# Triangular inverses of eight token tiles in one bundle, and planner estimates read off the trace

## The chip, the cores and the metric

The kernel runs on one core of one Trainium2 chip. The metric is the device time of one execution in microseconds. Its engines are named as the profile names them: PE (TensorE, with PEld for its weight loads), DVE (VectorE), ACT (ScalarE), POOL (GpSimd) and SP (SyncE, which here only issues DMAs). Each engine works through its own instructions in order, and engines wait for each other by semaphores.

## What is computed

One layer of a hybrid backbone: 1024 latent tokens and 256 context tokens of width 1024 are normed and projected, three mixers run on the projection (a gated linear recurrence, LRU; a gated delta rule, GDN; a state-space scan, SSD), their outputs are merged and projected, and a mixture of experts follows. The change lies in the GDN, whose core is, for a chunk of tokens of one head:

```python
dec = jnp.exp(jnp.where(incl, gcs[..., :, None] - gcs[..., None, :], -jnp.inf))
kb = kc * bc[..., None]
a_low = jnp.where(strict, jnp.einsum("bhid,bhjd->bhij", kb, kc) * dec, 0.0)
rhs = jnp.concatenate([vc * bc[..., None], kb * jnp.exp(gcs)[..., None]], axis=-1)
sol = lax.linalg.triangular_solve(eye + a_low, rhs, left_side=True, lower=True, unit_diagonal=True)
u, w = sol[..., :dv], sol[..., dv:]
v_new = u - jnp.einsum("bhcd,bhde->bhce", w, s)
o = (jnp.einsum("bhcd,bhde->bhce", qc * jnp.exp(gcs)[..., None], s)
     + jnp.einsum("bhij,bhje->bhie", attn, v_new))
s = s * jnp.exp(gcs[..., -1])[..., None, None] + jnp.einsum("bhcd,bhce->bhde", k_dec, v_new)
```

Eight heads are scanned in both directions, first over the context (from a zero state), then over the latents (from the context's final state). The kernel takes chunks of 128 tokens and replaces the triangular solve by the inverse of `I + B`, with `B` the strictly triangular matrix of a token tile and a direction.

## The kernel before

**Stages.** The stages follow each other: start (norms, transposes), LRU with the context's projections beside it (to about 586 us), GDN over the context (to 765), SSD (to 1268), GDN over the latents (to 2135), the merge and the output projection (to 2640), the experts. A stage's pools are opened and closed with it, and `drain` ends it.

**The order of work.** The main line of a stage is a list of jobs (`run`, line 350): projections of one block of 128 channels, each 48 products of 512 columns in single-precision-round format (`pj`). All else is side work, written as generators in the list `post`. After every three products (of a half block's row tile) `tick` (393) walks through `post` and lets each generator run to its next `yield`, if the planner's clock says that its last step is done. That order is fixed when the program is built: instructions go to the engines in it.

**The planner's clock.** `Clock` (145) holds an estimated time for each engine and each tile. `issue` (190) starts an instruction at the latest of its engine's time, its inputs' and its output buffer's, and adds `cost` (164). "Now" is TensorE's estimated time. A result counts as ready 0.1 us after its instruction. Costs before: a 512-column projection product 512 / 2400 = 0.213 us, a small single-precision product at least 0.06 us, a VectorE instruction 0.07 us (0.13 from PSUM) and 1.05 ns an element, for copies 0.53 ns; a scan counts as any other. `room` (386) waits for a PSUM bank by estimate, `take` (421) for a buffer by count, `until` holds up the main line for a flag, with the clock moved on to the next side step.

**GDN over the latents.** A head has two batches (`Batch`) of four token tiles. `gdn_jobs` (1583): the blocks K, Q, V of heads 0 and 1 are projected first; then for each head h its scans are added (`gdn_chain`, 1513, one generator a direction, eight steps each) and its output (`gdn_out`), the gate block GZ of h is projected, the main line waits for head h - 1's output, and K, Q, V of head h + 2 follow; a few merge gate blocks fill heads 5 to 7. `gdn_pre` of a head runs after that of the head before and after its K: for each batch `gdn_keys` (transposed keys, norms `sk`, factors `D`), `gdn_decays` (1192: POOL masks `gm`, two pairs of products `parg`, decays `dec`, `at` from queries, and, when a buffer `B` is free, eight DVE instructions `B<-pkk,D,dec` and two POOL masks), and then a side task `gdn_inverse` for that batch. After both batches it makes the values `vp` and sets `gpre`. A scan waits for the scan before, for `gpre` and for the inverses of both batches (`gi`).

**The inverse** (1267), for four token tiles in both directions at once: the diagonal 32-blocks of `B` go into `Bq`; the 16-blocks are inverted by substitution, 15 rounds of two shuffles of rows (`R<-Y`), a product (`R<-R,Bc`) and a difference (`Y<-Y,R`), all on DVE, in widths from 1 to 15 columns; then blocks are merged 16 to 32 to 64 to 128, each by two sets of small products on PE with copies by ACT and DVE between (`p1`, `py`, `p2`, `po` and `pz`, `p3`, `p4`; in the trace `p` and `P`). The result lies in `Yf`. Buffers for the latents: two of `B`, each given back after its inverse's `p3`; one of `Bq`, given back after `Bo`, ahead of the merges; one of `Yq`, given back at the end. The context works alike with batches of one token tile of four heads, and has two sets of buffers (`pars`), so two inverses at a time.

Of the kernel before, what the change touches and what calls it, by code (L numbers as in the profile page):

```python
# [136 lines left out]
CH2 = True  # L137
# [7 lines left out]
class Clock:  # L145
    """Estimated times (us) at which the engines and the tiles are free of the instructions issued so far; the order
    in which independent pieces of work are issued goes by them."""

    TABLES = (("Tanh", "Exp"), ("Gelu_apprx_tanh", "Tanh"), ("Silu", "Tanh"), ("Sqrt",), ("Sigmoid", "Tanh"))

# [67 lines left out]
class TimedPool:  # L218
    """a tile pool; keeps book of when the buffers that its tiles take over are free."""
# [50 lines left out]
class Core:  # L270
# [15 lines left out]
    # ---------------------------------------------------------------- consts  # L286
# [24 lines left out]
    def softplus(self, out, x, pool, shape, name):  # L311
        """max(x, 0) + log(1 + exp(-|x|)), the logarithm as 2 atanh(e / (2 + e))."""
# [39 lines left out]
    def run(self, jobs):  # L352
        """jobs: callables, or (weight block, kind, done); done(block, psum tile, is latent)."""
# [19 lines left out]
    def give(self, ps):  # L373
        """a projection's PSUM tile is not needed any more."""
# [754 lines left out]
    def gdn_fixed(self):  # L1129
# [4 lines left out]
        for y in self.Yf + self.Z64:  # L1134
            nc.vector.memset(y, 0.0)
# [1381 lines left out]
```

## Time and profile before

| | us |
|---|---|
| median of 3 runs | 3391.51 |
| lowest and highest | 3386.56, 3393.18 |
| span of the profiled execution | 3387.1 |

The profile is of one execution. The span runs from its first to its last instruction; the time of a run holds some microseconds around it (the median is 4.4 above this span). In the rows below, "busy" is the time in which an engine had an instruction under way, "idle before" what it stood ahead of the instructions of a group, with the engine and tile that ended it. Nearly all instructions carry line 256, that of the wrapper that records them, so tiles tell them apart. A single-precision product appears as two records. A tile's name is that of the program without its number: `p1`, `p2`, `p3` and `p4` are `p`, and `P1`, `P2`, `P3` are `P`.

### The profile page before, as it was taken

What the parts mean: (1) busy time and instruction counts of PE and PEld (TensorE: products, weight loads), DVE (VectorE), ACT (ScalarE), POOL (GpSimd) and SP (SyncE); (2) the same over time, 40 slices, a digit from 0 to 9 for tenths busy, and PEclk for the clock granted to TensorE, in tenths of its full rate; (3) what the DMA queues carried; (4) which work ended last, traced back from release to release, by engine and by line L of the source; (5) the groups of instructions that cost most, each with busy time, mean ns of one, the idle gap of its engine ahead of it and who ended that gap; (6) DMA issues with size and microseconds to landing.
All of it is one profiled execution on the core that took longest, in us unless ns stands there. A gap on an engine that the chain in (4) does not pass through costs nothing. (4 is left out here: it accounts for less than half of the span.)

```text
span 3387.1 us, 48583 instructions
## 1 busy us (share of the span) xinstructions
PE 2976.2 (88%) x18570; PEld 2345.0 (69%) x18570; DVE 2251.0 (66%) x5049; ACT 1553.5 (46%) x2188; POOL 772.1 (23%) x662
## 2 busy tenths in 40 slices
PE   7878789879799789879989999899988799999992
PEld 3657667667568557668777778677766588878882
DVE  4676765753744745887988885244544887787786
ACT  4556565424315324454444444311121576676674
POOL 1121221202612611112111111212110243333333
PEclk8989999979799799989999999999989799999996
DMA  4112222201002001001010111454443697887896
GB/s 187 63 56 78 74 76 78 78 24 50 13 32 75 7 26 62 28 21 35 22 34 27 34 47 65 153 195 174 150 145 136 260 361 290 310 337 287 321 354 235
DMA packets 105531, 423.12 MB, mean 125 GB/s; under 512 B 17224, under 2 KB 26568, under 8 KB 79696
## 3 DMA queue, kind: packets, MB, share of 16 engines
q1 hardware_dynamic: 79872, 372.17, 30.5%
q10 hardware_dynamic: 13968, 26.83, 2.1%
q0 software_dynamic: 11456, 21.00, 1.7%
q8 instruction: 147, 2.41, 0.3%
q14 instruction: 88, 0.72, 0.1%
HBM read 381.11 MB, written 59.79 MB: 130 GB/s over the span
## 5 line engine op out<-in xcount | busy, mean ns | idle before, releaser
L256 PE MATMUL pj<-hhi,whi 128*128 128x512 f32 x1488 | 643.8, 433 | 17.8 <-DVE kq L256 10.3
L256 PE MATMUL pj<-hhi,wlo 128*128 128x512 f32 x1488 | 597.7, 402 | 6.9 <-POOL wlo L256 3.7
L256 PE MATMUL pj<-hlo,whi 128*128 128x512 f32 x1488 | 597.4, 401 | 0.0
L256 DVE TENSOR_TENSOR wl<-raw,wh 128x2048 fp32r<-128x2048 f32 x188 | 447.9, 2403 | 103.4 <-ACT wh L256 101.1
L256 POOL TENSOR_TENSOR wlo<-raw,whi 128x1024 fp32r<-128x1024 f32 x78 | 197.1, 2527 | 1002.8 <-ACT whi L256 985.5
L256 ACT ACTIVATE wh<-raw 128x2048 fp32r<-128x2048 f32 x188 | 360.6, 1919 | 129.2 <-PE psu L256 103.2
L256 PEld LDWEIGHTS pj<-hhi,whi 128*128 128x128 f32 x1488 | 286.7, 193 | 77.8 <-issue 10.1
L256 PEld LDWEIGHTS pj<-hhi,wlo 128*128 128x128 f32 x1488 | 285.3, 192 | 78.4 <-POOL wlo L256 5.3
L256 PEld LDWEIGHTS pj<-hlo,whi 128*128 128x128 f32 x1488 | 287.6, 193 | 53.8 <-issue 3.2
L256 ACT ACTIVATE whi<-raw 128x1024 fp32r<-128x1024 f32 x145 | 152.8, 1056 | 293.6 <-PE pj L256 212.8
L256 PE MATMUL psu<-wl,xh 128*128 128x512 f32 x576 | 226.6, 393 | 2.9 <-DVE wl L256 2.9
L256 PE MATMUL psu<-wh,xh 128*128 128x512 f32 x576 | 229.1, 398 | 0.0
L256 PE MATMUL psu<-wh,xl 128*128 128x512 f32 x576 | 226.0, 392 | 1.1 <-DVE xl L256 1.1
L256 ACT ACT_TABLE_LOAD x147 | 188.6, 1283 | 77.0 <-DVE xt L256 32.2
L256 DVE TENSOR_TENSOR wlo<-raw,whi 128x1024 fp32r<-128x1024 f32 x67 | 87.8, 1310 | 185.0 <-ACT whi L256 185.0
L256 ACT ACTIVATE w<-ch,D 128x128 f32<-128x128 f32 x288 | 84.7, 366 | 161.6 <-PE ch L256 155.7
L256 POOL TENSOR_TENSOR yo<-yo,m 128x1024 f32<-128x1024 f32 x35 | 103.6, 2961 | 183.5 <-ACT yo L256 183.4
L256 PE MATMUL psg<-u,lw 128*128 128x512 f32 (+1 forms) x192 | 89.8, 605 | 55.5 <-issue 52.7
L256 PE MATMUL pj<-bh,whi 128*128 128x512 f32 x384 | 122.9, 402 | 12.0 <-DVE acc L256 6.5
L256 PE MATMUL pj<-bl,whi 128*128 128x512 f32 x384 | 122.2, 400 | 8.9 <-POOL bl L256 6.3
L256 PEld LDWEIGHTS psu<-wl,xh 128*128 128x128 f32 x576 | 109.0, 189 | 29.3 <-DVE wl L256 8.0
L256 PEld LDWEIGHTS psu<-wh,xl 128*128 128x128 f32 x576 | 108.8, 189 | 24.7 <-DVE xl L256 1.8
(455 smaller groups left out, 6295.5 us busy)
## 6 DMA issues: line engine op xcount, KB each, us to landing
raw<-in_w SPq DMA_DIRECT2D x188, 1024.0 KB, 6.8
raw<-in_w_in SPq DMA_DIRECT2D x119, 512.0 KB, 3.5
wr<-in_w_mod SPq DMA_DIRECT2D x32, 512.0 KB, 6.0
gate<-gt ACTq DMA_DIRECT2D x48, 256.0 KB, 2.0
raw<-in_w_branch SPq DMA_DIRECT2D x24, 512.0 KB, 3.6
st<-br SPq DMA_DIRECT2D x24, 512.0 KB, 5.5
gt<-gate SPq DMA_DIRECT2D x24, 512.0 KB, 4.5
wm<-in_w_mod SPq DMA_DIRECT2D x8, 1024.0 KB, 5.7
```

The source lines that it names most:

```text
L256: return f(*args, **kw)
```

## The change

`gdn_inverse` takes both batches of a head (in the context, both token tiles of four heads), so that each of its instructions covers eight token tiles. `gdn_pre` adds it once, after the keys and decays of both batches. The tiles double in their third dimension, and there is one set: `B` two buffers, both given back after `p3`; `Bq`, `Bo`, `Yq` and `Zq` one each, shared by what was in `Bc`, `Y`, `R` and `P1`; `Bq` is taken at the start and given back at the end. `Z64` holds one direction for each quadrant, so half of the `pz` products and of the copies around them go. `Bo` is made ahead of the substitution, a yield comes after every second round instead of every third, and `p4` waits for a bank. `small_tiles` keeps one tile less, and the switch `CH2` goes (its branch stays for the latents). `Clock.cost` gets new lines, and the lag after an instruction depends on its engine.

```diff
+    LAG = {"tensor": 0.21, "vector": 0.11, "scalar": 0.12, "gpsimd": 0.1, "sync": 0.1}
...
         if eng == "tensor":
             if op == "transpose":
-                return 0.12
+                return 0.11
             c = kw["rhs"].free_size()
-            return c / 2400 if kw["rhs"].dtype == F32R else max(4 * c / 2400, 0.06)
+            if kw["rhs"].dtype == F32R:
+                return c / 2400 + 0.014
+            rows = kw["lhsT"].partition_size()
+            if "tile_position" in kw:
+                return 0.024 if rows == 32 else 0.055
+            return max(c / 600, 0.11)
+        psum = any(a.space == PSUM for a in ins)
         if eng == "vector":
             if op == "reciprocal":
                 return 0.07 + n * 6.3e-3
+            if op == "tensor_tensor_scan":
+                return 0.08 + n * 2.08e-3
             if op == "tensor_reduce":
-                n = ins[0].free_size()
-            psum = any(a.space == PSUM for a in ins)
-            fast = op in ("tensor_copy", "tensor_scalar") and not psum
-            return (0.13 if psum else 0.07) + n * (0.53e-3 if fast else 1.05e-3)
+                return 0.08 + ins[0].free_size() * 1.04e-3
+            if op == "stream_shuffle":
+                return 0.13 + n * 1.0e-3
+            if op in ("tensor_copy", "tensor_scalar", "memset"):
+                c = 0.14 if len(ins) > 1 else 0.09
+                return c + n * (1.04e-3 if psum else 0.52e-3)
+            c = 0.15 if op == "scalar_tensor_tensor" and len(ins) > 2 else 0.09
+            return c + n * 1.04e-3
         if eng == "scalar":
             f = str(kw.get("func")).split(".")[-1]
-            c = 0.13 + 0.75e-3 * n
+            c = (0.08 if psum else 0.12) + 0.09 * max(0, len(ins) - 1) + 0.83e-3 * n
+            if kw.get("accum_out") is not None:
+                c += 0.2
             if any(f in t for t in self.TABLES) and f not in self.table:
                 self.table = next(t for t in self.TABLES if f in t)
-                c += 1.28
+                c += 1.38
             return c
         if op == "indirect_dma_start":
             return 1.0
-        return 0.1 + n * {"tensor_tensor": 2.2e-3, "affine_select": 1.05e-3}.get(op, 3.5e-3)
+        if op == "affine_select":
+            return 0.12 + n * 0.9e-3
+        return 0.15 + n * (2.25e-3 if op == "tensor_tensor" else 3.5e-3)
...
-            t += 0.1
+            t += self.LAG[eng]
...
-        self.pars = 1 if lat else 2
-        b |= {f"{n}{p}": 2 if n == "B" and lat else 1 for p in range(self.pars)
-              for n in ("B", "Bq", "Bo", "Bc", "Y", "R", "Yq", "Zq", "P1")}
+        b |= {"B": 2} | dict.fromkeys(("Bq", "Bo", "Yq", "Zq"), 1)
...
         for bt in bts:
             yield from self.gdn_keys(bt, keys=not lat)
             yield from self.gdn_decays(bt)
-            self.add(self.gdn_inverse(bt))
+        self.add(self.gdn_inverse(bts))
...
+        def t(name, c):
+            return g.tile([P, 2, 8, c], F32, tag=name, name=name)
...
+        yield from self.take(g, "Bq")
+        Bq = t("Bq", 32)
+        for i, bt in enumerate(bts):
+            for q in range(4):
+                r = slice(32 * q, 32 * q + 32)
+                o = Bq[r, :, 4 * i:4 * i + 4, :]
...
+        Bc = flat(t("Zq", 32))[:, 0:256].rearrange("p (d e c) -> p d e c", d=2, c=16)
...
+        yr = flat(t("Bq", 32)).rearrange("p (n d e c) -> p n d e c", n=2, d=2, c=16)
+        Y, R = yr[:, 0], yr[:, 1]
...
-            nc.vector.tensor_tensor(out=Rv, in0=Rv, in1=Bv, op=ALU.mult)
+            Rv, Yv = Rw[:, :, j:], Yw[:, :, j:]
+            nc.vector.tensor_tensor(out=Rv, in0=Rv, in1=Bw[:, :, j:j + 1].to_broadcast([P, 16, 16 - j]), op=ALU.mult)
             nc.vector.tensor_tensor(out=Yv, in0=Yv, in1=Rv, op=ALU.subtract)
-            if s % 3 == 2:
+            if s % 2:
                 yield
...
-                nc.tensor.matmul(pz[rb, e, :], lhsT=Y32[rb, d, e, :], rhs=P2[rb, e, :], start=True, stop=True,
-                                 tile_position=(32 * b, 32 * b))
+                if b // 2 == d:
+                    nc.tensor.matmul(pz[rb, e, :], lhsT=Y32[rb, d, e, :], rhs=P2[rb, e, :], start=True, stop=True,
+                                     tile_position=(32 * b, 32 * b))
...
+        P3 = flat(t("Bq", 32)).rearrange("p (e c) -> p e c", c=64)
         nc.scalar.activation(out=P3, in_=p3, func=AF.Copy)
-        g.used[f"B{bt.par}"] -= 1
+        g.used["B"] -= 2
         yield
-        p4 = aux.tile([P, 4, 64], F32, tag="aux", name="p4")
+        yield from self.room()
+        p4 = aux.tile([P, 8, 64], F32, tag="aux", name="p4")
...
-        g.used[f"Yq{bt.par}"] -= 1
+        g.used["Bq"] -= 1
         yield
-        self.flags.add(("gi", bt.id))
+        for bt in bts:
+            self.flags.add(("gi", bt.id))
```

## Rows read from the trace of the kernel before

**Rows 1.** The page's head and its section 1: busy time, share, instructions.

```profile
span 3387.1 us, 48583 instructions
PE 2976.2 (88%) x18570; PEld 2345.0 (69%) x18570; DVE 2251.0 (66%) x5049; ACT 1553.5 (46%) x2188; POOL 772.1 (23%) x662
```

**Rows 2.** Windows by stage: length, busy us and instructions of each engine, clock, DMA.

```profile
90.00:586.00 496.00, 426.84 (x2027) 330.12 (x2027) 335.82 (x399) 282.44 (x356) 89.63 (x38) 0.93 0.21 70
586.00:765.00 179.00, 144.04 (x1584) 117.20 (x1584) 112.72 (x583) 60.31 (x129) 24.23 (x28) 0.85 0.16 54
765.00:1268.00 503.00, 442.35 (x1844) 324.75 (x1843) 267.35 (x413) 174.05 (x306) 170.59 (x183) 0.91 0.10 33
1268.00:2135.00 867.00, 793.30 (x7940) 649.57 (x7939) 688.51 (x2880) 399.47 (x763) 145.16 (x244) 0.96 0.11 37
```

**Rows 3.** Windows inside the latent heads' stage; columns as in rows 2.

```profile
1340.00:1540.00 200.00, 166.81 (x2002) 132.47 (x2003) 176.51 (x803) 87.22 (x170) 29.48 (x52) 0.91 0.08 24
1540.00:2060.00 520.00, 484.99 (x5218) 398.43 (x5218) 442.27 (x1861) 245.77 (x493) 93.11 (x161) 0.98 0.11 34
```

**Rows 4.** Waits of PE, 1268 to 2135: total us, times, longest us.

```profile
PE ch L256 <- DVE o L256: 25.1, 26, 3.7
PE pj L256 <- DVE kq L256: 10.3, 3, 6.8
```

**Rows 5.** Timeline of DVE, rounds of a substitution: start us, length us, instruction.

```profile
1423.40 0.22 DVE L256 STREAM_SHUFFLE R<-Y 128x56 f32<-128x56 f32 x1
...
1424.42 0.23 DVE L256 STREAM_SHUFFLE R<-Y 128x60 f32<-128x60 f32 x1
...
1434.25 0.16 DVE L256 STREAM_SHUFFLE R<-Y 128x4 f32<-128x4 f32 x1
...
1434.99 0.17 DVE L256 STREAM_SHUFFLE R<-Y 128x8 f32<-128x8 f32 x1
```

**Rows 6.** Timeline of DVE, behind a substitution.

```profile
1428.16 0.73 DVE L256 TENSOR_SCALAR Yq<-Y,s 128x64 f32<-128x64 f32 x4
1428.80 0.48 DVE L256 TENSOR_SCALAR Bo<-Bq,s 128x128 f32<-128x128 f32 x2
```

**Rows 7.** Groups of instructions, 1300 to 2110: busy us, mean ns, idle before.

```profile
L256 DVE STREAM_SHUFFLE R<-Y 128x4 f32<-128x4 f32 (+14 forms) x480 | 72.7, 193 | 0.5
L256 PE MATMUL p<-Zq,Bo 32*32 32x32 f32 x1024 | 12.3, 196 | 2.9 <-DVE Zq L256 2.9
L256 PE MATMUL pz<-P,Y 32*32 32x32 f32 x512 | 12.2, 203 | 11.4 <-DVE B L256 4.9 <-DVE at L256 4.4 <-DVE gz L256 1.2
```

**Rows 8.** Timeline of DVE: inverses of heads 4 and 5, and first state updates.

```profile
1722.58 0.48 DVE L256 TENSOR_SCALAR Bo<-Bq,s 128x128 f32<-128x128 f32 x2
...
1723.44 0.59 DVE L256 COPY Bq<-B 32x256 f32<-32x256 f32 x2
...
1784.12 0.85 DVE L256 TENSOR_SCALAR Yf<-p 64x256 f32<-64x256 f32 x2
...
1798.35 0.34 DVE L256 SCALAR_TENSOR_TENSOR S<-S,ge,ch 128x128 f32<-128x128 f32 x1
...
1876.70 0.85 DVE L256 TENSOR_SCALAR Yf<-p 64x256 f32<-64x256 f32 x2
...
1895.65 0.34 DVE L256 SCALAR_TENSOR_TENSOR S<-S,ge,ch 128x128 f32<-128x128 f32 x1
```

**Rows 9.** Timeline of POOL, masks of B: head 4's second batch, then head 5.

```profile
1709.83 0.64 POOL L256 TENSOR_SCALAR_AFFINE_SELECT B<-B 128x512 f32<-128x512 f32 x1 [13.09 <-DVE B L256]
...
1771.24 0.63 POOL L256 TENSOR_SCALAR_AFFINE_SELECT B<-B 128x512 f32<-128x512 f32 x1 [2.34 <-DVE B L256]
...
1804.05 0.64 POOL L256 TENSOR_SCALAR_AFFINE_SELECT B<-B 128x512 f32<-128x512 f32 x1 [15.83 <-DVE B L256]
```

**Rows 10.** Groups of DVE instructions in the LRU stage, 90 to 586.

```profile
L256 DVE TENSOR_TENSOR_SCAN ea<-ea,gate 128x256 f32<-128x256 f32 (+2 forms) x24 | 46.4, 1946 | 0.3
```

**Rows 11.** Waits of PE in the LRU stage, 90 to 586.

```profile
PE psg L256 <- issue: 52.7, 7, 13.8
```

More of the change, by code (lines that the diff above doesn't have):

```diff
@@ L136 @@
 CM = None
-CH2 = True
 SPLIT = True
@@ L1137, in gdn_fixed @@
         self.ch = self.chb.rearrange("p (a b) -> p a b", b=P)
-        if self.pars == 1 and not CH2:
-            self.ch2 = self.ch[:, 2:4]
-        if self.pars == 1 and CH2:
+        if lat:
             self.chb2 = self.aux.hold("ch")
@@ L1223, in gdn_decays @@
             yield
-        yield from self.take(g, f"B{bt.par}")
-        bt.B = B = g.tile([P, 2, 4, P], F32, tag=f"B{bt.par}", name="B")
+        yield from self.take(g, "B")
+        bt.B = B = g.tile([P, 2, 4, P], F32, tag="B", name="B")
         yield from self.room()
@@ L1265, in gdn_pre, with gdn_inverse @@
         self.flags.add(done)
[L1267 removed]
+    def gdn_inverse(self, bts):
         nc = self.nc
@@ L1320, in quads @@
             for d in range(2):
-                for e in range(4):
+                for e in range(8):
                     for q in range(4):
@@ L1327, in gdn_inverse @@
         yield from self.room()
-        p1 = aux.tile([P, 2, 4, 64], F32, tag="aux", name="p1")
-        quads(p1[:, :, :, 0:32], Bo, Zq)
-        P1 = g.tile([P, 2, 4, 32], F32, tag=f"P1{bt.par}", name="P1")
-        nc.scalar.activation(out=P1, in_=p1[:, :, :, 0:32], func=AF.Copy)
+        p1 = aux.tile([P, 2, 8, 32], F32, tag="aux", name="p1")
+        quads(p1, Bo, Zq)
+        P1 = t("Bq", 32)
+        nc.scalar.activation(out=P1, in_=p1, func=AF.Copy)
         yield
         yield from self.room()
-        py = aux.tile([P, 2, 4, 64], F32, tag="aux", name="py")
-        quads(py[:, :, :, 0:32], P1, Yq)
-        Y32 = g.tile([P, 2, 4, 32], F32, tag=f"Bo{bt.par}", name="Y32")
-        nc.vector.tensor_tensor(out=Y32, in0=Yq, in1=py[:, :, :, 0:32], op=ALU.subtract)
-        Z32 = g.tile([P, 2, 4, 32], F32, tag=f"Zq{bt.par}", name="Z32")
-        nc.vector.transpose(out=Z32.rearrange("p d e c -> p (d e c)"), in_=Y32.rearrange("p d e c -> p (d e c)"))
-        yield
-        if bt.lat and bt.h > 1:
-            yield from self.wait(("gch", bt.h - 2))
-        bt.Yf = Yf = self.Yf[bt.id % 4]
-        Z64 = self.Z64[bt.par]
+        py = aux.tile([P, 2, 8, 32], F32, tag="aux", name="py")
+        quads(py, P1, Yq)
+        Y32 = t("Bo", 32)
+        nc.vector.tensor_tensor(out=Y32, in0=Yq, in1=py, op=ALU.subtract)
+        Z32 = t("Zq", 32)
+        nc.vector.transpose(out=flat(Z32), in_=flat(Y32))
+        yield
+        if bts[0].lat and bts[0].h > 1:
+            yield from self.wait(("gch", bts[0].h - 2))
+        Yf = self.Yf[bts[0].id // 2 % 2]
+        for i, bt in enumerate(bts):
+            bt.Yf = Yf[:, :, 4 * i:4 * i + 4, :]
+        Z64 = self.Z64
         for q in range(4):
@@ L1349, in gdn_inverse @@
                 nc.vector.tensor_copy(out=Yf[r, :, :, r], in_=Y32[r])
[L1350 removed]
+                nc.scalar.activation(out=Z64[r, :, c], in_=Z32[r, q // 2], func=AF.Copy)
             else:
                 nc.scalar.activation(out=Yf[r, :, :, r], in_=Y32[r], func=AF.Copy)
[L1353 removed]
+                nc.vector.tensor_copy(out=Z64[r, :, c], in_=Z32[r, q // 2])
         yield from self.room()
[L1356 removed]
+        p2 = aux.tile([P, 8, 32], F32, tag="aux", name="p2")
         pairs = ((0, 0, 1), (0, 2, 3), (1, 1, 0), (1, 3, 2))
[L1358 removed]
+        for e in range(8):
             for d, a, b in pairs:
                 ra, rb = slice(32 * a, 32 * a + 32), slice(32 * b, 32 * b + 32)
[L1361 removed]
+                nc.tensor.matmul(p2[rb, e, :], lhsT=B(d, e)[ra, rb], rhs=Z32[ra, d, e, :], start=True, stop=True,
                                  tile_position=(32 * a, 32 * b))
[L1363 removed]
+        P2 = t("Bq", 32)[:, 0]
         nc.scalar.activation(out=P2, in_=p2, func=AF.Copy)
@@ L1366, in gdn_inverse @@
         pb = yield from self.bank("po")
-        po = pb[:, 0:P].rearrange("p (a b) -> p a b", b=32)
+        po = pb[:, 0:2 * P].rearrange("p (a b) -> p a b", b=32)
         yield from self.room()
-        pz = aux.tile([P, 4, 32], F32, tag="aux", name="pz")
-        for e in range(4):
+        pz = aux.tile([P, 8, 32], F32, tag="aux", name="pz")
+        for e in range(8):
             for d, a, b in pairs:
@@ L1379, in gdn_inverse @@
             ca = slice(32 * (a % 2), 32 * (a % 2) + 32)
-            nc.vector.tensor_scalar(out=Z64[rb, d, :, ca], in0=pz[rb], scalar1=-1.0, scalar2=None, op0=ALU.mult)
+            if b // 2 == d:
+                nc.vector.tensor_scalar(out=Z64[rb, :, ca], in0=pz[rb], scalar1=-1.0, scalar2=None, op0=ALU.mult)
             nc.scalar.activation(out=Yf[ra, d, :, rb], in_=po[ra], func=AF.Copy, scale=-1.0)
@@ L2273, in phase1 @@
                     c.aux.free(c.chb)
-                    if CH2:
-                        c.aux.free(c.chb2)
+                    c.aux.free(c.chb2)
             if "moe" in stages:
```

84 lines of the change are left out of this document (36 added, 48 removed).

## The prediction

> **What bounds the kernel now.** I read the page's head first: the span is 3387.1 us and TensorE is busy for 88% of it [rows 1], so the kernel as a whole is near TensorE's limit, and a cheaper VectorE is worth something only where TensorE stands still. The share is an average over stages, so the next view is the table by stage [rows 2]. The planner's estimates act in all four of those stages; the triangular inverses run in two, the context heads (586 to 765) and the latent heads (1268 to 2135). In the latent heads TensorE is busy for 793.3 of 867 us and VectorE for 688.5, so at most 74 us of TensorE's idle time can be won there. Cut further [rows 3], the stage falls in two. From 1340 to 1540 VectorE is busy for 176.5 of 200 us, TensorE for 166.8 at a granted clock of 0.91: VectorE is the bound. From 1540 to 2060 TensorE is busy for 485.0 of 520 us, VectorE for 442.3: both are near it, TensorE nearer. The waits view names what TensorE's idle time ends on: VectorE, led by the scan's products behind the output `o` (25.1 us) and a projection behind the convolution `kq` (10.3 us) [rows 4].
>
> **Part 1, eight token tiles in one bundle.** The sixteen latent inverses become eight, the four of the context two. A substitution has 15 rounds of two shuffles, a product and a difference on VectorE. A round of the shortest (4 elements a shuffle) takes 1434.99 - 1434.25 = 0.74 us and one of 56 elements 1424.42 - 1423.40 = 1.02 us [rows 5]; the 14 lengths in units of four elements from 1 to 14 give 0.72 us + 0.0215 us a unit, so 0.18 us of an instruction is fixed. Fifteen rounds: 15 x 0.72 + 120 x 0.0215 = 13.4 us for four tiles, 26.8 us for two such, and 15 x 0.72 + 240 x 0.0215 = 16.0 us for eight. Saved: 10.8 us a head, in half of the 480 shuffles [rows 7] and of the products and differences that go with them. Around the rounds two inverses have 54 VectorE instructions and a bundle 27 (the copies into `Bq` stay four, those of `pz` fall from eight to two, all others halve; `Z64` keeps one direction a quadrant, so its copies hold half the elements). Four `Yq` instructions take 0.73 us and two `Bo` 0.48 [rows 6]; with 0.13 us fixed, 27 x 0.13 = 3.5 us. Together 14.3 us a head: 114 us of VectorE in the latent stage (688.5 to about 574) and 29 us in the context's 112.7 [rows 2].
>
> [...]
>
> On TensorE only `pz` shrinks, by half of 12.2 us at most [rows 7]: 0 to 6 us, taken as 3. ScalarE issues fewer and longer copies; at 399 of 867 us it bounds nothing [rows 2].
>
> At nothing stand the new wait for a PSUM bank ahead of `p4` (a bank is held back by at most one other step, about 1 us a head on the loop below if that cover is gone), the smaller tiles, and the dropped switch `CH2`, whose branch was taken anyway. No DMA and no queue of SP moves with the inverses.
>
> **What of the 114 us lies on the path.** In 1340 to 1540, 2.5 heads of inverses run; 2.5 x 14.3 = 36 us of VectorE go, and TensorE's idle 33 us is what they can become. [...] In 1540 to 2060 the heads follow each other at the distance of the ends of their inverses, 1876.7 - 1784.1 = 92.6 us, and each scan's first state update comes 14 to 19 us behind that end [rows 8]: a head starts when its inverse is there. TensorE's work in that distance is 485.0 / 520 x 92.6 = 86.4 us, and no period can fall below it. So the steady part can give 6.2 us a head, 5.6 heads, 35 us at most; how much of it depends on the order in which a bundle may start.
>
> **Part 2, what the bundle waits for.** Before, a head's first inverse starts as soon as its own `B` stands, and the second follows when `Bq` is given back, 1722.58 to 1723.44 [rows 8], its substitution beside the first one's merges. Now the bundle waits for both `B`, keeps both until its third product (`p3`) and `Bq` to its end, so the next head's `B` cannot be written meanwhile. Queued behind that are the rest of the next head's preparation (its `pq` product, the second half's keys and decays, and the values behind `gpre`), then its inverse, then its scan. From rows: first `B` to second `B` is 1804.05 - 1771.24 = 33 us, and second `B` to the inverse's end 1784.1 - 1709.8 = 74 us [rows 8, 9]; in sequence 107 us a head under today's load. The lower end is what is left if waiting in VectorE's queue shrinks with its load, from 442 / 520 = 85% to (92.6 x 0.85 - 14.3) / 92.6 = 70%. Of the 107 us about 16 + 10 us are then the bundle's own VectorE work, and if the other 81 shrink by the load's ratio, 0.82, they become 66: 92 us; if by the queue's ratio ((0.70 / 0.30) / (0.85 / 0.15) = 0.41), the 86.4 us of TensorE bind. I take 89, between these: 3.6 us a head, 20 us over the 5.6 heads.
>
> The latent stage: 25 + 20 = 45 us, between 25 + 0 and 33 + 35. In the context stage both `B` of the second group come free together instead of one by one; TensorE is busy for only 144.0 of 179 us [rows 2], so latency decides there: 14 us less substitution and merging in each of two bundles in sequence, less a second decay, some 10 us, that no longer hides beside the first inverse: 2 x 14.3 - 2 x 10 = 9, taken as 5, between -12 and 20.
>
> **Part 3, the estimates.** They change no instruction outside the inverses, only which piece is issued when. Two are far off before: a scan of 1280 elements is estimated at 1.41 us, and the 24 scans of the LRU stage take 46.4 us [rows 10] where the old line gives 23 and the new one 45; a 32 x 32 product is estimated at 0.06 us, and 1024 records, two for a product, are busy for 12.3 us [rows 7], 0.024 each, as the new line has it. With the scan too cheap, the LRU gates' first product is put into TensorE's queue before VectorE has its input: TensorE stands for 52.7 us in seven such waits [rows 11]. A pair of scans was 2.8 us too short in each block: 7 x 2.8 = 20 us less standing, of which projections in the same queue give back none, but a projection's estimate rises too (512 columns from 0.213 to 0.227 us), which brings side steps forward by some 7% and takes a part of it. I take 12, between 0 and 25. In the SSD stage no estimate is off by such an amount; 0, between -15 and 15. What is after 2135 has its order from the program's text but for a few side steps: 0.
>
> **The sum.** 45 + 5 + 12 + 0 = 62 us off the profiled execution: 3387.1 - 62 = 3325. The median of the runs shown is 4.4 us above that execution's span, so the forecast is 3329 us.
>
> **Rivals.**
> - Slower, the handover of `B`: if VectorE's queue is not what stretches the preparation and the inverse (if it is the planner's step by step issue beside TensorE's projections), the loop stays at 107 us. Then each of the 5.6 heads is 14 us longer, 81 us, against 25 + 5 + 12 won elsewhere: +39, 3430 us. It decides from 92.6 us a head on, and half of the way (100 us) still gives about 3391. For it: each step waits for a tick between projection products. Against it: VectorE is the releaser of nearly all TensorE waits in the stage [rows 4], and it loses a sixth of its work.
> - The whole cover: latent 68, context 20, LRU 25, SSD 5: 118 us, 3273. For it: TensorE idles for 35 + 69 + 61 us in the context, LRU and SSD stages [rows 2]. Against it: each of those is taken at its best.
> - The estimates wash out and the bundle does not do what it says: the steady period is TensorE's own and its stalls move instead of vanishing, SSD loses what LRU wins; what stays is 0 to 7 us: 3388 us.
>
> **How the numbers follow.** The forecast, with its terms anywhere between -20 and -95, has 0.60; the whole cover 0.14; no change 0.09; the handover 0.17, of which 0.05 end below 3385 because the loop lands under 100 us. A measurement of this kernel tells about 0.2% from no change, 6.8 us. Faster: 0.60 + 0.14 + 0.05 = 0.79; within: 0.09; slower: 0.12. The range takes in the whole cover's end, and of the handover the part up to a loop near 101 us: 3268 to 3398.
>
> **What would show it.** Right: substitution rounds of 0.76 to 1.36 us in place of two of 0.74 to 1.02; VectorE near 575 us in the latent stage; TensorE's waits on VectorE there halved; ends of inverses 86 to 92 us apart; the gates' waits in the LRU stage near 30 us. Wrong: ends 95 us apart or more with POOL's `B` masks following `p3` at once (the handover), or new TensorE waits in the SSD stage as long as those gone from LRU (the estimates).

## The result, and the profile after

The changed kernel takes 3412.5 us (median of 4 runs, 3406.9 to 3413.6) against 3391.7 for the kernel before on the same chip: a ratio of 1.0063, with a 95% interval from 1.0051 to 1.0075. It is 0.6% slower, where 3329 us, 1.8% faster, was predicted. The profiled execution has a span of 3411.9 us, 24.8 us longer than before's 3387.1 [rows 1]. First the head of its page, with busy time, share and instructions of each engine:

```profile
span 3411.9 us, 46610 instructions
PE 2964.3 (87%) x18250; PEld 2354.7 (69%) x18250; DVE 2125.8 (62%) x3875; ACT 1542.1 (45%) x2084; POOL 765.0 (22%) x661
```

VectorE lost 125 us of work (114 + 29 = 143 were forecast) and 1174 instructions. Nothing of that reached the span. Next the windows by stage, columns as in [rows 2], cut where the stages of this kernel end:

```profile
90.00:585.00 495.00, 422.55 (x2002) 328.01 (x2003) 331.69 (x393) 283.03 (x358) 89.11 (x38) 0.92 0.21 67
585.00:773.00 188.00, 143.54 (x1522) 118.01 (x1521) 88.79 (x352) 54.87 (x107) 22.78 (x27) 0.79 0.17 56
...
1286.00:2166.00 880.00, 790.00 (x7707) 662.73 (x7707) 588.17 (x1943) 393.05 (x683) 143.29 (x244) 0.92 0.11 38
```

In the latent heads VectorE's work fell from 688.5 to 588.2 us, but the stage is 10 us longer (by the marks of the table below) and TensorE's granted clock is 0.92 instead of 0.96. The next two windows answer [rows 3], moved by the 18 us by which the stage begins later:

```profile
1358.00:1558.00 200.00, 175.01 (x1797) 145.57 (x1796) 142.66 (x476) 89.72 (x153) 33.85 (x56) 0.92 0.08 26
1558.00:2078.00 520.00, 464.90 (x4732) 394.11 (x4730) 370.81 (x1276) 239.57 (x430) 86.49 (x157) 0.91 0.11 35
```

At the stage's beginning TensorE is busy for 8 us more than before. In the steady part it stands for 55 us instead of 35, at 0.91 instead of 0.98, while VectorE is busy for only 71%. Neither engine is full over this stretch. TensorE's waits in the whole stage, in total, times and longest, to be read against [rows 4]:

```profile
PE ch L275 <- DVE o L275: 34.8, 32, 2.7
PE p L275 <- DVE Zq L275: 21.0, 12, 3.8
```

The scan's wait grew from 25.1 to 34.8 us, and that on `Zq`, the last instruction of the substitution, from 2.9 to 21.0. The loop shows in the timeline. First POOL's masks of `B` (first mask of each), as in [rows 9]:

```profile
1713.49 0.64 POOL L275 TENSOR_SCALAR_AFFINE_SELECT B<-B 128x512 f32<-128x512 f32 x1 [34.74 <-DVE B L275]
...
1737.93 0.64 POOL L275 TENSOR_SCALAR_AFFINE_SELECT B<-B 128x512 f32<-128x512 f32 x1 [4.95 <-DVE B L275]
...
1811.88 0.64 POOL L275 TENSOR_SCALAR_AFFINE_SELECT B<-B 128x512 f32<-128x512 f32 x1 [34.52 <-DVE B L275]
```

and VectorE's timeline of the same bundle, from the end of one inverse (`Yf<-p`) to the end of the next, as in [rows 8]:

```profile
1714.31 1.38 DVE L275 TENSOR_SCALAR Yf<-p 64x512 f32<-64x512 f32 x2
...
1754.78 0.61 DVE L275 TENSOR_SCALAR Bo<-Bq,s 128x256 f32<-128x256 f32 x2
...
1758.58 0.18 DVE L275 STREAM_SHUFFLE Bq<-Bq 128x8 f32<-128x8 f32 x1
...
1759.34 0.19 DVE L275 STREAM_SHUFFLE Bq<-Bq 128x16 f32<-128x16 f32 x1
...
1790.20 0.71 DVE L275 STREAM_TRANSPOSE Zq<-Yq 128x512 f32<-128x512 f32 x1
...
1812.70 1.38 DVE L275 TENSOR_SCALAR Yf<-p 64x512 f32<-64x512 f32 x2
```

These inverses end 1812.7 - 1714.3 = 98.4 us apart; over the eight heads the distances are 94 to 102, 98.5 on the mean. Before, the mean was 93.6, with distances from 58 to 135; the 92.6 of the prediction is one of them. First `B` to second `B` is 1737.9 - 1713.5 = 24 us, second `B` to the end 75 us: in sequence 99 us, the distance. That is the chain of the rival that I called the handover of `B`, and its sign (`B` of the next head directly behind `p3`, ends 95 us or more apart). The last windows cut one bundle into its preparation, its substitution and its merges (in the next head VectorE has 31.7 of 35 and 9.1 of 22 us in the last two):

```profile
1737.00:1757.00 20.00, 19.56 (x124) 17.31 (x123) 17.92 (x53) 12.97 (x26) 4.29 (x11) 1.00 0.09 27
1757.00:1792.00 35.00, 26.27 (x208) 22.10 (x211) 31.53 (x138) 13.82 (x24) 4.89 (x8) 0.85 0.05 16
1792.00:1814.00 22.00, 20.60 (x479) 16.72 (x469) 9.81 (x23) 8.52 (x15) 1.27 (x2) 0.77 0.17 57
```

While the substitution runs VectorE is busy for 31.5 of 35 us: about 18 are the bundle's own, and about 12 belong to the scan and the output of the head before, which fall into the same stretch. In the merges behind it VectorE has 9.8 of 22 us. TensorE has the opposite: it stands for 9 of 35 us while VectorE is full, and for 1.4 of 22 in the merges.

A scan waits for its inverse and for the scan before it. Which of the two ended later changed. The last state update of the scan of head 3, before and after:

```profile
1787.72 0.34 DVE L256 SCALAR_TENSOR_TENSOR S<-S,ge,ch 128x128 f32<-128x128 f32 x1
```

```profile
1787.41 0.34 DVE L275 SCALAR_TENSOR_TENSOR S<-S,ge,ch 128x128 f32<-128x128 f32 x1
```

Before, head 4's inverse had ended at 1784.1 [rows 8], ahead of that scan; so it was in five of the seven heads that follow another, by 4 to 17 us. After, the inverse ends at 1812.7, 25 us behind the scan, and by 22 to 31 us in all seven. A scan of the steady part got shorter, from about 80 to 60 us between its first and last state update, and each head's first one now comes 12 to 15 us behind its inverse: the heads follow the inverses.

By stage, from the traces' marks (the clearing of `Yf` for the context, the last store of a context state, the clearing of `Yf` for the latent heads, the last gated output), in us:

| | LRU and ahead | context | SSD | latent | behind |
|---|---|---|---|---|---|
| before | 579.5 | 178.9 | 509.3 | 869.3 | 1250.2 |
| after | 585.1 | 187.5 | 513.6 | 879.4 | 1246.4 |
| predicted change | -12 | -5 | 0 | -45 | 0 |
| measured change | +5.6 | +8.6 | +4.3 | +10.1 | -3.8 |

### The profile page after: what moved, and what is told of

Its sections match the earlier page's. It is cut to its first block, busy times and chain, and to the rows that moved or that the text cites. A ratio compares the mean times of both kernels' runs of the same rounds, so it can differ in the third digit from the quotient of the medians.

```text
span 3411.9 us, 46610 instructions
## 1 busy us (share of the span) xinstructions
PE 2964.3 (87%) x18250; PEld 2354.7 (69%) x18250; DVE 2125.8 (62%) x3875; ACT 1542.1 (45%) x2084; POOL 765.0 (22%) x661
## 5 line engine op out<-in xcount | busy, mean ns | idle before, releaser
L275 PE MATMUL pj<-hhi,whi 128*128 128x512 f32 x1488 | 636.8, 428 | 9.5 <-ACT whi L275 5.5
L275 PE MATMUL psg<-u,lw 128*128 128x512 f32 (+1 forms) x192 | 89.9, 602 | 50.7 <-issue 44.6
```

The costliest lines, as they stand in the source:

```text
L275: return f(*args, **kw)
```

## The experiments

The theories at first were **H**, the handover; **C**, the estimates order the work worse; **S**, the substitution's small pieces wait for turns between projection products. All ratios are to the kernel before on the same chip, with 95% intervals. Times in us of different runs come from several chips; on them the kernel before took 3388.9 to 3391.7 us.

### Each part alone

The kernel before with the new class `Clock`, and the changed kernel with the old one.

> The kernel before with the new estimates alone (the inverses of four token tiles and their tiles as before). Theory H (the bundle's handover of B costs the time: both B of a head are held until the third product, so the next head's preparation and its inverse run in sequence, 24 us from B to B plus 77 us to the end of the inverse, about 99 us a head): ends of the latent inverses stay 91 to 94 us apart, the latent stage is within 5 us of before, and only the +8 us seen in the LRU and SSD stages of the changed kernel remain: 3385 to 3403 us. Theory C (the estimates order the work worse): the ends are 97 us or more apart and the time is 3405 to 3415. Theory S (a step by step issue stretches the substitution, 36 us for 16 us of VectorE's work): as H here.

> The changed kernel with the old estimates (the bundle of eight alone). Theory H: ends of the latent inverses 96 to 102 us apart, the LRU stage as before; 3400 to 3412 us. Theory C: ends 92 us apart or less, 3340 to 3390. Theory S: as H here, 3400 to 3412, with the substitution still 30 us or longer in each head.

The estimates alone: 3434.3 us, 1.0125 (1.0109 to 1.0140). The bundle alone: 3392.6 us, 1.0007 (0.9998 to 1.0016). For the bundle the loop is H's: its inverses end 97 us apart on the mean with the old estimates too, and it wins nothing; its time lies 7 us below H's range. For the estimates C is right that they cost time, against my expectation, but not in its range and not in its mark (ends 97 us apart or more): with separate inverses they cost 43 us, 26 of them in the latent stage and 13 behind it, while the inverses end 95 us apart on the mean. In the trace of the estimates alone the latent stage is 895 us long:

```profile
1274.00:2169.00 895.00, 808.31 (x7958) 674.33 (x7958) 693.96 (x2880) 402.96 (x766) 144.85 (x244) 0.94 0.11 37
```

with VectorE's work as before (694 us). The two causes don't add: together they cost 21 us.

### A third buffer of B

The control makes room for it by taking `at` from six buffers to four, with a wait ahead of its product and both given back at the end of a head's scan:

```diff
-        b |= {..., "at": 6, ...}
+        b |= {..., "at": 4, ...}
...
+            yield from self.take(g, "at")
...
+        self.gd.used["at"] -= 2
```

The run proper adds

```diff
-        b |= {"B": 2} | ...
+        b |= {"B": 3 if lat else 2} | ...
```

> Control for the next run: the changed kernel with four instead of six buffers of the tile at (and a wait for one of them). All theories: the first half's at of the next head but one waits for the end of a scan that ends some 25 us before B is handed over, so nothing moves: within 6 us of the changed kernel, 3406 to 3420.

> As the control, with a third buffer of B in the latent stage, so that the first half's B of the next head can be written while the running inverse still holds its two. Theory H: the 24 us between the two B leave the loop; the new bound is 3 us from the third product to the second B plus 77 us, or TensorE's 86 to 88 us a head; ends 86 to 91 us apart, 55 to 85 us less in the latent stage, 3330 to 3360 us. Theory C: ends stay 97 us or more apart, 3400 to 3415. Theory S (the chain of a bundle is itself 99 us whatever comes first, for lack of ticks): ends 94 to 99 us apart, 3385 to 3412.

Control: 3417.6 us, 1.0082 (1.0068 to 1.0096), as expected. Three `B`: 3397.6 us, 1.0019 (1.0010 to 1.0028), 20 us less than the control, but not the 55 to 85 of H; the time falls into the range of S, the ends do not. The ends of inverses alternate, 59 to 69 and 123 to 134 us apart, 92 on the mean. First masks of successive `B`, POOL's timeline of this run:

```profile
1704.37 0.63 POOL L275 TENSOR_SCALAR_AFFINE_SELECT B<-B 128x512 f32<-128x512 f32 x1 [10.23 <-DVE B L275]
...
1729.93 0.64 POOL L275 TENSOR_SCALAR_AFFINE_SELECT B<-B 128x512 f32<-128x512 f32 x1 [4.10 <-DVE B L275]
...
1779.63 0.64 POOL L275 TENSOR_SCALAR_AFFINE_SELECT B<-B 128x512 f32<-128x512 f32 x1 [15.01 <-DVE B L275]
...
1810.31 0.63 POOL L275 TENSOR_SCALAR_AFFINE_SELECT B<-B 128x512 f32<-128x512 f32 x1 [13.89 <-DVE B L275]
```

The pairs are still 26 and 31 us apart. Each first `B` comes behind its `at`, and `at` now waits for the end of a scan (last state updates at 1698 and 1767): the buffer that paid for the third `B` is likely to have become the next limit. The run speaks for H but doesn't measure it.

### Both halves prepared ahead

This takes away what lies between the two `B` instead: keys, decays and `at` of both halves of a head first, then `B` twice. `gdn_decays` now ends with `at`; the new `gdn_b` holds the wait for `B`, the product `pkk`, and `B` with its mask. It needs a second `dec`, paid with one buffer of the gates' tile `gt` in this stage.

```diff
         for bt in bts:
             yield from self.gdn_keys(bt, keys=not lat)
             yield from self.gdn_decays(bt)
+            if not lat:
+                yield from self.gdn_b(bt)
+        for bt in bts if lat else []:
+            yield from self.gdn_b(bt)
         self.add(self.gdn_inverse(bts))
```

> The changed kernel, but in the latent stage the keys, decays and at of both halves of a head are made before either B is asked for (two buffers of dec; for their space one buffer of the gates' tile gt in this stage), so that after the running inverse's third product only the two B themselves are left, some 5 us instead of 24. at keeps its six buffers. Theory H (the handover sets the loop): 5 + 77 = 82 us, below TensorE's 86, so ends of inverses 86 to 91 us apart and 60 to 85 us off the changed kernel: 3330 to 3355 us. Theory H2 (the run with three buffers of B stayed at 97 us a head because something else, the scan of the head before and its four at, held the next B): the same, since at is not short here. Theory S (a bundle's own chain stretches to whatever time there is): 94 us or more apart, 3390 to 3412.

> The same with the estimates of the kernel before. If the estimates cost on their own about the 20 us that lie between the changed kernel (3413) and the bundle alone (3393): 20 us less than the run beside it, LRU, context and SSD stages as before: theory H 3310 to 3340, theory S 3372 to 3392. If the estimates only act through the loop: the same time as the run beside it.

3373.1 us, 0.9949 (0.9935 to 0.9962): 39 us less than the changed kernel, and less than the kernel before. First masks of `B`:

```profile
1689.80 0.63 POOL L275 TENSOR_SCALAR_AFFINE_SELECT B<-B 128x512 f32<-128x512 f32 x1 [18.40 <-DVE B L275]
...
1697.23 0.64 POOL L275 TENSOR_SCALAR_AFFINE_SELECT B<-B 128x512 f32<-128x512 f32 x1 [0.15 <-DVE B L275]
...
1773.63 0.64 POOL L275 TENSOR_SCALAR_AFFINE_SELECT B<-B 128x512 f32<-128x512 f32 x1 [9.67 <-DVE B L275]
...
1782.50 0.63 POOL L275 TENSOR_SCALAR_AFFINE_SELECT B<-B 128x512 f32<-128x512 f32 x1 [7.02 <-DVE B L275]
```

The gap between the two `B` fell from 24 to 7 and 9 us, and the latent stage from 879 to 836 us. These 43 us are what the handover costs the stage (no run takes the buffer of `gt` alone). They are less than the 60 to 85 expected. In the loop it is 55 us, from 98.5 to 90.6 a head over seven heads, with a longer inverse; from the last inverse's end to the last gated output it takes 15 us longer than in the changed kernel. And in three of seven heads the scan before again ends behind the inverse: there a shorter handover could not have started the scan earlier. The windows of the stage, and of one substitution and its merges:

```profile
1286.00:2122.00 836.00, 772.77 (x7705) 651.78 (x7705) 589.77 (x1943) 381.38 (x676) 150.45 (x244) 0.96 0.12 40
1711.00:1756.00 45.00, 39.70 (x227) 32.63 (x228) 40.72 (x157) 21.47 (x36) 10.06 (x18) 0.98 0.09 27
1756.00:1776.00 20.00, 16.30 (x536) 14.38 (x536) 14.23 (x44) 10.18 (x23) 2.10 (x5) 0.88 0.02 4
```

Preparation of the next head has moved beside the substitution, which takes 45 us instead of 35, with VectorE busy for 40.7 of them. The ends are 90.6 us apart on the mean of all eight heads; TensorE, which stands for 63 us in the stage instead of 90, has its clock back at 0.96.

With the old estimates the same kernel takes 3377.1 us, 0.9966 (0.9953 to 0.9978). The expected 20 us less were a miss: the stages ahead of the latent heads end 12 us earlier, and the latent stage is 15 us longer (851). The new estimates cost in the early stages and pay in the latent stage of this kernel.

### Why the substitution is long

```diff
-            if s % 2:
+            if s % 5 == 4:
                 yield
```

> The changed kernel with a step of the substitution of five rounds instead of two, so that it is issued in three pieces instead of seven. Theory S (the pieces wait for a turn between projection products, which stretches 16 us of VectorE's work to 36): the substitution falls to 22 to 25 us, the ends of inverses to 86 to 92 us apart, 3340 to 3375 us. Theory D (VectorE itself is full while the substitution runs, 31.5 of 35 us, because the scan of the head before falls into the same stretch, and it idles in the merges after it, 9.8 of 22 us): the scan's steps now wait behind longer pieces, the substitution gets a few us shorter and the scan as much longer: 3400 to 3425.

3404.9 us, 1.0042 (1.0030 to 1.0055). From `Bo` to `Zq`, as in the timeline above (35 us there):

```profile
1737.77 0.61 DVE L275 TENSOR_SCALAR Bo<-Bq,s 128x256 f32<-128x256 f32 x2
...
1777.22 0.71 DVE L275 STREAM_TRANSPOSE Zq<-Yq 128x512 f32<-128x512 f32 x1
```

39 us in three pieces in this head. Over the eight heads the substitution takes 27 to 40 us, 35 on the mean, against 33 to 42, 37 on the mean, in the changed kernel: fewer turns don't bring it to the 22 to 25 of S, and S falls. That fits the PE timeline of the changed kernel: between 1776.2 and 1798.7 no projection product starts, so for the last 14 us of that substitution there is none to wait for. D is left, by its time and because VectorE is full just then (31.5 of 35 us in the changed kernel, 35.3 of 39 here); that the scan grows as much as the substitution shrinks was not measured.

### The context stage

Two runs: four buffers of `B` there on top of both halves prepared ahead, and the kernel before's inverses of four token tiles, two side by side, in the context alone. The second is compared with a run that has the same estimates: old ones up to the SSD stage's end, new ones in the latent stage.

```diff
+                c.clk.new = True
                 c.run(J["gdn"])
```

> The kernel with both halves prepared ahead (3373), with four buffers of B instead of two in the context stage, so that the second group of heads there need not wait for the first group's bundle. Theory H for the context (second group's states 15 us later than before because its B wait for the first group's third product): the last states are stored at 755 to 762 instead of 773 us, 10 to 18 us less, 3355 to 3363. If the context's end is set by the bundle's own length: 3368 to 3378.

> Both halves prepared ahead (3373), with the estimates of the kernel before up to the SSD stage's end and the new ones from the latent stage on. If the estimates act stage by stage: LRU, context and SSD end at 1273 us as with the old estimates (12 us earlier than with the new), the latent stage takes 836 us as with the new: 3355 to 3367. If what the latent stage takes depends on the state in which it begins rather than on the estimates in it: 3365 to 3385.

> The run beside it, with the kernel before's inverses of four token tiles in the context stage (two of them side by side) and bundles of eight in the latent stage alone. If the context lost its 9 us to one bundle after the other (one Bq, 52 to 56 us a bundle) where two inverses ran side by side: the last context state is stored at 757 us instead of 766, 7 to 11 us less than the run beside it. If its end is set by anything else: the same within 3 us.

Four `B`: 3379.5 us, 0.9963 (0.9950 to 0.9976), against 3373.1, 0.9949 (0.9935 to 0.9962), without: nothing won, a miss. VectorE's timeline:

```profile
661.44 2.15 DVE L275 SCALAR_TENSOR_TENSOR B<-pkk,D,dec 128x128 f32<-128x128 f32 x8
...
686.69 1.41 DVE L275 TENSOR_SCALAR Yf<-p 64x512 f32<-64x512 f32 x2 [4.79 <-PE p L275]
...
741.99 1.41 DVE L275 TENSOR_SCALAR Yf<-p 64x512 f32<-64x512 f32 x2 [4.79 <-PE p L275]
```

The second group's `B` stand at 664, 23 us ahead of the first bundle's end, but its inverse ends 55 us behind that end: it waits for `Bq`, of which there is one. In the context the bundle's own length decides, not `B`.

Mixed estimates: 3363.0 us, 0.9924 (0.9910 to 0.9937), as expected from adding stages. With inverses of four in the context: 3354.5 us, 0.9900 (0.9887 to 0.9914), 8.5 us less; its context stage takes 179 us again, against 188. Ends of the context's inverses, first with a bundle each, then with four each:

```profile
668.99 1.40 DVE L305 TENSOR_SCALAR Yf<-p 64x512 f32<-64x512 f32 x2
...
732.72 1.41 DVE L305 TENSOR_SCALAR Yf<-p 64x512 f32<-64x512 f32 x2 [4.79 <-PE p L305]
```

```profile
657.35 0.85 DVE L305 TENSOR_SCALAR Yf<-p 64x256 f32<-64x256 f32 x2
...
681.96 0.85 DVE L305 TENSOR_SCALAR Yf<-p 64x256 f32<-64x256 f32 x2
...
717.49 0.86 DVE L305 TENSOR_SCALAR Yf<-p 64x256 f32<-64x256 f32 x2 [0.18 <-PE p L305]
...
726.18 0.86 DVE L305 TENSOR_SCALAR Yf<-p 64x256 f32<-64x256 f32 x2 [0.72 <-PE p L305]
```

Two side by side end 7 us ahead of the second bundle. This kernel is faster than both the one before and the changed one.

### The estimates

Lines taken back one by one: the projection's, the lags, and the small products'. The theories: **P**, the projection line; **L** and **K**, the costs of VectorE and ScalarE; **G**, the lags; **T**, TensorE's lines; **Q**, the small products.

```diff
-                return c / 2400 + 0.014
+                return c / 2400
```

> The changed kernel with one line of the estimates taken back: a 512-column product of the projections at 0.213 us again instead of 0.227. Theory P (the longer projection estimate moves every side step earlier in TensorE's queue, ahead of its input): the 20 us that the estimates cost beside the bundle come back, 3390 to 3400. Theory L (the estimates of VectorE, ScalarE and the lags after an instruction are what moves the steps): no change, 3405 to 3418.

> The kernel before with the new estimates except that same line. Theory P: most of the 43 us that the estimates alone cost come back, 3391 to 3403. Theory L: 3425 to 3440. Between: both have a share.

```diff
-    LAG = {"tensor": 0.21, "vector": 0.11, "scalar": 0.12, ...}
+    LAG = {"tensor": 0.1, "vector": 0.1, "scalar": 0.1, ...}
```

> The changed kernel with the lags after an instruction as before (0.1 us for each engine, instead of 0.21 after TensorE, 0.11 and 0.12 after VectorE and ScalarE). Since the run with the old projection estimate got slower by 18 us, the projection line was worth something (it brings side steps forward), and another line of the new estimates costs over 20. Theory G (the longer lag after TensorE makes each step that follows a product look ready later, so chains of small steps, the scan's and the inverse's, are issued later than they could be): 15 to 30 us come back, 3383 to 3400. Theory K (the costs of VectorE's and ScalarE's instructions do it): within 7 us, 3405 to 3420.

> The kernel with both halves prepared ahead (3373) with the same old lags. Theory G: faster, 3345 to 3365. Theory K: 3366 to 3380.

> The kernel before with the new estimates from the latent stage on alone. If the estimates themselves order the latent stage of separate inverses worse: 895 us there instead of 869 and 12 more behind it, 3418 to 3432. If most of the 43 us came from another state at that stage's beginning: 3385 to 3405.

The next takes the costs of VectorE, ScalarE and GpSimd from the class before, and the last two are

```diff
-                return 0.024 if rows == 32 else 0.055
+                return 0.06
```

> The kernel before with the new estimates of TensorE's instructions and the new lags alone; VectorE, ScalarE and GpSimd as before. Theory K (the new costs of VectorE and ScalarE order the side steps worse): 3380 to 3405. Theory T (TensorE's small products and lags do): 3420 to 3440.

> The kernel before with the new estimates, but the 32- and 64-row products of the inverses at 0.06 us again (now 0.024 and 0.055). Theory Q (the planner's clock, which is TensorE's estimate, now gains 7.5 us less a head from 208 products, so side steps come up later beside the projections; the projection line, which adds 2.7 us a head, worked the other way): most of the latent stage's 26 us come back, 3395 to 3412. If it is none of the lines singly: 3425 to 3440.

> The kernel with inverses of four in the context, bundles in the latent stage and the new estimates there alone (3354), with the same line taken back in the latent stage. Theory Q: side steps earlier, 5 to 15 us less, 3339 to 3350. If not: 3350 to 3365.

| run | us | ratio to before (interval) | the same without the edit |
|---|---|---|---|
| old projection line, changed kernel | 3430.6 | 1.0113 (1.0098 to 1.0128) | 3412.5 |
| old projection line, estimates alone | 3444.7 | 1.0160 (1.0147 to 1.0173) | 3434.3 |
| old lags, changed kernel | 3405.4 | 1.0052 (1.0039 to 1.0065) | 3412.5 |
| old lags, both halves prepared | 3386.1 | 0.9984 (0.9975 to 0.9993) | 3373.1 |
| before, new estimates in the latent stage | 3421.9 | 1.0099 (1.0085 to 1.0115) | 3388.9 |
| before, new TensorE lines and lags | 3434.2 | 1.0130 (1.0114 to 1.0145) | 3388.9 |
| old small products, estimates alone | 3446.6 | 1.0167 (1.0153 to 1.0181) | 3434.3 |
| old small products, context of four | 3368.8 | 0.9936 (0.9923 to 0.9950) | 3354.5 |

P falls: taking the line back makes both kernels slower, by 18 and 10 us. G falls as a rule: the old lags give 7 us in one kernel (the intervals overlap) and cost 13 in the other. By stage, in the changed kernel they make the latent stage 16 us shorter, as G has it, and the LRU stage 8 us longer; with both halves prepared the LRU stage is 10 us longer and the latent stage 8. Q falls: 12 and 14 us slower. What stands: with separate inverses the new estimates order the latent stage itself worse (895 us although only that stage has them), and TensorE's lines with the lags do it without those of the other engines. Which of them, or only their combination, stays open; the lags alone were not tried with separate inverses. The loss shows in the scans: with the new estimates in the latent stage those of heads 3 to 5 take 82, 88 and 96 us from first to last state update, before 80, 82 and 78.

In the LRU stage more can be said. TensorE's waits there: of the changed kernel; of the estimates alone with the old projection line; and of TensorE's lines and the lags alone:

```profile
PE psg L275 <- issue: 44.6, 6, 13.9
```

```profile
PE psg L276 <- issue: 28.5, 6, 9.7
PE pjc L276 <- ACT gate L276: 10.9, 5, 5.4
PE pss L276 <- DVE sst L276: 7.6, 2, 5.0
PE psg L276 <- ACT whi L276: 4.1, 1, 4.1
```

```profile
PE psg L304 <- issue: 37.1, 8, 10.4
```

Without the projection line the gates' waits come down from 52.7 us [rows 11] to 28.5, near the 30 predicted; but 22.6 us of other waits appear, and the stage ends 3 us earlier than before, not 20. With it the gates' waits are 44.6 and the stage ends 6 us later than before. The scan line was not taken back by itself. Taken back with all costs of VectorE, ScalarE and GpSimd, it leaves waits of 37.1 us, less than the 44.7 of all new estimates; taking back the lags in the changed kernel raises them from 44.6 to 54.6. So what brings the gates' waits down here is the lags, and the scan line is not seen to do it.

## Why the prediction was wrong

**VectorE's saving was right in kind and a little too large.** A round of two shuffles of 8 elements is 1759.34 - 1758.58 = 0.76 us, the figure given. The stage's work fell by 688.5 - 588.2 = 100 us, 12.5 a head against 14.3.

**"I take 89" failed.** The step that put the loop between 92 and 86.4 us let its elapsed times shrink with VectorE's average load. The loop measured 98.5 on the mean. The load did fall, from 85% to 71%, as forecast (70%), and the gap of the two `B` shrank from 33 to 24 us; but the second `B` to the end stayed at 75 us (74 before), with a bundle in the place of one inverse. The load while the chain passed through VectorE's queue was not the average: 31.5 of 35 us in the substitution, 9.8 of 22 in the merges. Before, one inverse's merges ran beside the other's substitution. The handover had the chain, the sign and the side right, with 99 us in place of 107; I gave it 0.17 for a reason (VectorE loses a sixth of its work) that doesn't touch a chain. The condition that I had set for it, the planner's issue between projection products, is for the substitution theory S, which fell; for the preparation it was not tested. In so far its side was luck. The prepared-ahead run shows the price: 43 us of the latent stage.

**The reading "a head starts when its inverse is there" failed too.** The rows show an inverse's end 14 to 19 us ahead of a scan's first state update. They leave out the end of the scan before, which lay 4 us behind that end in both heads shown. So the heads before followed their scans at least as much as their inverses, and in these heads a shorter inverse alone could not have brought them closer. What the steady part would have done with shorter scans and inverses as early as before, no run shows.

**The latent stage in its parts.** No run shows the 25 us that the sum has for the beginning: TensorE is busy there for 175.0 us instead of 166.8, 8 more, but no head comes earlier: counted from the clearing of `Yf`, head 3's inverse ends at 426 us before and 428 after. From there to head 7's inverse 366 became 399 us, 33 more, where 20 less were forecast. From that inverse to the last gated output 78 became 52 us, 25 less, which the sum did not have: without it the stage would be 35 us longer and not 10. Together 27 + 53 - 25 = 55 us off the forecast. The granted clock is 0.92 in place of 0.91 at the beginning, and 0.91 in place of 0.98 in the steady part.

**The context** was +8.6 instead of -5. "14 us less substitution and merging in each of two bundles in sequence" is nearly true of VectorE's work (112.7 to 88.8 us); the step missed that the context kernel before had two inverses side by side and the bundle has one `Bq`. The runs put 8.5 us on that.

**The LRU stage** was +5.6 instead of -12. The projection line works against the gain, as said, and costs the stage 6 us. The other term failed: that the scan line takes the gates' waits down is not borne out (37.1 us without it, 44.7 with it, other costs changing with it), and the lags, which do take them down, were not in the sum. 20 us of shorter waits were taken as 20 us of time, and where 24 us of them went, other waits filled all but 3.

**The estimates elsewhere** were set to nothing because "They change no instruction outside the inverses". With separate inverses they cost 26 us in the latent stage. Beside the bundle the stage is 876 us with the old and 879 with the new: there the loop hides the order, and the prediction's zero held by accident.

By stage: 55.1 (latent), 17.6 (LRU), 13.6 (context), 4.3 (SSD) and -3.8 behind make the 87 us between the forecast of the profiled span, 3325, and the 3411.9 measured.

## What to carry to other kernels

Before bundling two chains of small steps into one, lay the chain of one bundle end to end from the trace, with the buffers that it holds until its last reader, and compare that with the period; work saved on an engine counts only if this sum stays below it. Look also, in every head, at which of the things that a step waits for ends last: a mean distance between two ends does not tell. Where the sum is longer, move what can be made ahead in front of the scarce buffer: here that turned 3412 us into 3373, and with the old estimates kept in the early stages and two inverses side by side in the context it became 3354. A planner's better durations are not a better order: take each change of them as an experiment of its own.

## What the runs showed of the hardware

The granted clock did not go by the amount of idle time alone. From 1540 to 2060 before, TensorE stands for 35 of 520 us, at 0.98; in the same part after, for 55 us, at 0.91; but in the first part before it stands for 33 of 200 us, a larger share, at the same 0.91 [rows 3]. Nor did it go by the longest single wait, which is 4.9 us in the steady part before and 3.8 after. What differs there is that in the changed kernel the waits of a head follow each other: the lower of the two levels that the trace shows, 0.50 and 1.00, lasts 20 us at a time in four heads of the steady part, where before it lasts 3 to 7 us at a time. TensorE's timeline of the changed kernel around such a piece:

```profile
1775.92 0.40 PE L275 MATMUL pj<-hlo,whi 128*128 128x512 f32 x1
1776.16 0.39 PE L275 MATMUL pj<-hhi,wlo 128*128 128x512 f32 x1
...
1800.12 0.63 PE L275 MATMUL pj<-hhi,whi 128*128 128x512 f32 x1
1800.54 0.63 PE L275 MATMUL pj<-hlo,whi 128*128 128x512 f32 x1
...
1804.06 0.39 PE L275 MATMUL pj<-hhi,whi 128*128 128x512 f32 x1
1804.29 0.40 PE L275 MATMUL pj<-hlo,whi 128*128 128x512 f32 x1
```

and two windows, in the piece and behind it, with the granted clock after the five busy times:

```profile
1790.00:1795.00 5.00, 3.13 (x198) 2.90 (x202) 2.82 (x8) 0.80 (x2) 0.00 (x0) 0.50 0.01 3
1804.00:1812.00 8.00, 8.00 (x93) 6.57 (x93) 1.38 (x6) 1.25 (x3) 0.12 (x1) 1.00 0.16 55
```

Projection products start 0.24 us apart ahead of the piece. Between 1776.2 and 1798.7 none starts: the kernel holds its main line for the output of the head before, and the products come back 2.7 us behind the transposes of that output. With small steps alone TensorE stands for 8.7 of the 16 us from 1776 to 1792, and from 1781 to 1802 the granted clock is 0.51 on the mean, nearly all of it at 0.50. The projection products in this stretch start 0.42 us apart; from 1804 on they are 0.23 apart again, at a granted clock of 1.00. So here the six projection products from 1798.7 to 1801.4, right behind the chain of small steps, take longer too: 0.42 - 0.23 = 0.19 us each, an estimated 1.1 us for the six.
